# Low halves of w_down's split weights: a subtraction on VectorE, or a negated copy on ScalarE and an accumulating DMA

## The chip, the cores and the metric

One core of a Trainium2 chip runs one launch of the kernel. The metric is the device time of that launch in microseconds (us), median of three runs; the engines are TensorE (PE), VectorE (DVE), ScalarE (ACT), GpSimd (POOL) and SyncE (SP), and SP issues all DMAs of the kernel before.

## What is computed

One decoder layer for 512 prompt tokens and 64 sample tokens (576 columns in all, D_MODEL 1024, D_FF 4096). Only the last two lines matter here:

```python
h1 = x + jnp.concatenate([oa, ob], axis=-1) @ w_o
hid = jnp.square(jax.nn.relu(rmsnorm(h1, norm2_g) @ w_up))
y = h1 + hid @ w_down
```

All inputs and outputs are float32. The kernel multiplies in the type `fp32r`, which keeps fewer bits, and so splits each operand into a high part (the value rounded to `fp32r`) and a low part (the value minus its high part). A product is three matmuls: high by high, high by low, low by high.

## The kernel before

Matrices lie transposed: 128 features on the partitions, tokens along the free dimension, in two halves of 288 (`HALF`). One matmul is 128x128 weights by 288 tokens.

The whole kernel is written as generators (tasks) that a planner, `Flow`, interleaves at build time: `fl.op` books an instruction on an engine with a cost in ns, and the engine queues get their instructions in the order of the planned start times. The planner's costs set the order only; on the chip semaphores decide when each instruction starts.

The last stage is the MLP. `order` (L372 to L376) lists its weight groups: sixteen units `("u", u)` of w_up, and from u = 3 on, behind every odd u, the four chunks `("d", c, i)` of a block c of w_down (behind u = 15 the eight chunks of c = 6 and 7). A d chunk is 128 x 1024 floats (512 KB) and serves four k tiles by 256 output features. So there are seven places at which PE goes from a u unit to a run of d chunks, with 32 d chunks in all.

How a weight chunk reaches PE:

- `loader` (L393) issues its DMA from SP into a raw tile (`wr` in the profile, use `mr`, at most four at a time in this stage).
- `group_splitter` (L421) walks through `order` and takes tiles of the use `mw`, of which six may live at a time (L337). A product of a u unit takes one tile, which holds both parts of a 128 x 512 sum of blocks; a d chunk takes two, `h` and `l`, and only when it has both does it start `whole` (L485). `rel("mr")` and `rel("mw")` hand tiles back.
- `whole` writes the high part on ACT (`act(h, x)`), the low part on DVE (`tt(l, x, f(h), OP.subtract)`), marks the pair in `wready`, and frees the raw tile.
- `mlp_gemm` (L1888) is PE's program: for a u unit of u >= 2 the seven products of `up` (L1803) in the order `PO` = 1, 2, 6, 5, 7, 3, 4 of 12 matmuls each, for a d chunk two times `gemm` (L1006), 48 matmuls.

`gemm` uses the parts of a chunk in this order, so the low part is first read by the third matmul:

```python
mm(p, wh[:, s], x_h[:, j, c0:c1], j == 0, False, extra=extra)
mm(p, wh[:, s], x_l[:, j, c0:c1], False, False, extra=extra)
mm(p, wl[:, s], x_h[:, j, c0:c1], False, j == nk - 1, extra=extra)
```

In a u unit, ACT also copies the accumulators out after products 1, 6 and 5 (`up_out`, L1832, rows `uq<-pg`), and product 3 may start to accumulate onto product 5's accumulator only when that copy is done (`seen`, L1764, used at L1811). Products 3 and 4 end the unit.

With six `mw` tiles, the tiles of the first d chunk of a run are those of products 2 and 6 of the unit ahead; so its `h` can be written when product 6 is done, and products 5, 7, 3 and 4 (48 matmuls) stand between that and the chunk's own first matmul.

Of the kernel before, what the change touches and what calls it, by code (L numbers as in the profile page):

```python
# [13 lines left out]
OP = mybir.AluOpType  # L14
# [198 lines left out]
def hymba_step(ctx: ExitStack, tc: tile.TileContext, a):  # L213
    nc = tc.nc
    fl = Flow()
# [21 lines left out]
    def rel(*uses):  # L237
        def go():
            for u in uses:
                live[u] -= 1  # L240
                live[home[u]] -= 1
        fl.do(go)
# [5 lines left out]
    def size(x):  # L248
        n = 1
        for q in x.shape[1:]:  # L250
            n *= q
        return n
# [14 lines left out]
    def act(out, in_, func=AF.Copy, bias=0.0, scale=1.0, accum=None, mark=None, extra=0):  # L267
        cost = (51 if on_psum(in_) else 93) + size(in_) / 1.2 + extra
        cost += (93 if accum is not None else 0) + (93 if ap(bias) or ap(scale) else 0)
        fl.op("ACT", cost, lambda: nc.scalar.activation(out, in_, func, bias=bias, scale=scale,  # L270
                                                        accum_out=accum), mark)

    def dve(emit, out, in_, extra=0, fast=False, mark=None):
        fast = fast and not on_psum(out) and not on_psum(in_)
        fl.op("DVE", 68 + size(in_) / (1.92 if fast else 0.96) + extra, emit, mark)

    def tt(out, x, y, op, mark=None):
        dve(lambda: nc.vector.tensor_tensor(out, x, y, op=op), out, x, mark=mark)  # L278
# [41 lines left out]
    def dma(dst, src, mark=None, slow=1):  # L320
        fl.op("SP", 4 * slow * size(dst) * dst.shape[0] / 360.0, lambda: nc.sync.dma_start(dst, src), mark)  # L321

    go_on = lambda t: None

    f = lambda t: t.bitcast(F32)
# [32 lines left out]
    items, chunk, ready = [], {}, {}  # L358
# [43 lines left out]
    def mark(d, k, v):  # L402
        c = fl.cur
        fl.do(lambda: d.update({k: (v, c.t)}))
# [7 lines left out]
    wready = {}  # L412
# [8 lines left out]
    def group_splitter():  # L421
        yield lambda: "split_o" in done
        for g in order:
# [8 lines left out]
            if g[0] == "d":  # L432
                h = yield from get("mw", MID, "mw", F32R)
                l = yield from get("mw", MID, "mw", F32R)
                fl.spawn(whole(g, r[0], h, l))
                yield 0
                continue
# [46 lines left out]

    def whole(g, x, h, l):  # L485
        act(h, x)
        yield 0
        tt(l, x, f(h), OP.subtract)
        mark(wready, (g, 0), (h, l))
        rel("mr")  # L490
        yield 0

    def weights(g, k):
# [1547 lines left out]
```

## Time and profile before

| | us |
|---|---|
| median of 3 runs (816.64 to 821.53) | 818.16 |
| the profiled execution: its own time | 818.95 |
| its span, first to last instruction | 817.2 |
| PE busy | 792.2 (97%) |
| DVE busy | 568.7 (70%) |
| ACT busy | 348.3 (43%) |
| POOL busy | 109.4 (13%) |
| DMA queue of SP, share of 16 engines | 36.6% |

The profile page shows the span in 40 slices of 20.4 us, each digit the busy share of a slice in tenths; the rows of the groups below give a line of the kernel (L262 is the helper that issues every matmul, L270 every ScalarE instruction, L278 every two-operand VectorE instruction, L321 every DMA of SP), the operation, and the tile written and read. In the chain of waits each step is followed back to what released it. A row of the timeline merges equal instructions that follow each other; `[0.22 <-PE pg L262]` at its end says how long the engine was idle before it and what ended that. PE's clock was granted in full in the slices of the MLP.

### The profile page before, as it was taken

The page shows a single profiled execution, that of the slowest core. Times are in us where ns is not written, and L with a number is a line of the kernel's source. Part 1 is how long each engine was busy: PE and PEld are TensorE (multiplying, and loading weights), DVE is VectorE, ACT ScalarE, POOL GpSimd, SP SyncE. Part 2 cuts the span into 40 slices and gives each one's busy share as a digit, 9 for nine tenths or more (in the row PEclk, how much of TensorE's full clock was granted, in tenths as well). Part 3 has the DMA queues.
Part 4 walks back from the last instruction along what each step waited for, and adds up shares of the span by engine and source line. Part 5 has one row for each costly group of instructions (what it writes and reads, how often), then busy time and mean ns, then how long its engine had stood idle before and what let it go on. Part 6 is the DMA issues. An engine that isn't in the chain of part 4 may idle for free.

```text
span 817.2 us, 15699 instructions
## 1 busy us (share of the span) xinstructions
PE 792.2 (97%) x6323; PEld 728.1 (89%) x6323; DVE 568.7 (70%) x1250; ACT 348.3 (43%) x728; POOL 109.4 (13%) x128
## 2 busy tenths in 40 slices
PE   8989998999999999999997999999999999999998
PEld 8968877879778687778997999999999999999998
DVE  4366269888776785668798886768677676867642
ACT  5547453655242134443466543515343351534400
POOL 3443224134224000121000000000000000000000
PEclk9999999999999999999999999999999999999999
DMA  7732320106686799122221141404123130412302
GB/s 270 125 112 77 123 68 31 55 27 245 211 345 185 273 319 327 49 93 81 104 104 52 59 150 52 129 27 155 53 94 113 52 129 27 155 53 95 112 30 87
DMA packets 49864, 99.05 MB, mean 121 GB/s; under 512 B 12864, under 2 KB 26304, under 8 KB 49792
## 3 DMA queue, kind: packets, MB, share of 16 engines
q1 hardware_dynamic: 49792, 98.05, 36.6%
q8 instruction: 50, 0.82, 0.4%
q14 instruction: 22, 0.18, 0.1%
HBM read 88.15 MB, written 9.69 MB: 120 GB/s over the span
## 4 chain that ended last, share of the span: by engine, by line
PE 73%; issue 9%; DVE 7%; DMA 6%; ACT 2%; SPq 2%; POOL 1%; POOLq 0%; ACTq 0%; DVEq 0%
PE pg L262 53%; PE pa L262 7%; DVE y L285 2%; SPq L321 2%; PE cha L262 2%; DMA wr<-in_wk_dram 2%; DMA morekv<-in_cv_dram 1%; PE os L262 1%; PE ptp L265 1%; DMA morekv<-in_ck_dram 1%; PE cs L262 1%; DMA silvz<-dU 1%; PE sc L262 1%; PE s L262 1%; PE sn L262 1%
## 5 line engine op out<-in xcount | busy, mean ns | idle before, releaser
L262 PE MATMUL pg<-hid,mw 128*128 128x288 f32 x1536 | 204.7, 295 | 0.0
L262 PEld LDWEIGHTS pg<-hid,mw 128*128 128x128 f32 x1536 | 203.9, 188 | 0.0
L262 PE MATMUL pg<-xf,mw 128*128 128x288 f32 x1368 | 186.0, 297 | 4.6 <-ACT xf L270 3.8
L262 PEld LDWEIGHTS pg<-xf,mw 128*128 128x128 f32 x1368 | 183.7, 189 | 5.6 <-ACT xf L270 4.3
L278 DVE TENSOR_TENSOR h<-pg,h 128x288 f32<-128x288 f32 x160 | 72.5, 455 | 94.6 <-PE pg L262 93.8
L270 ACT ACTIVATE mw<-wr 128x512 fp32r<-128x512 f32 (+1 forms) x82 | 62.9, 791 | 70.8 <-PE pg L262 70.1
L262 PE MATMUL pg<-xh,wh 128*128 128x288 f32 x256 | 78.0, 305 | 0.0
L262 PE MATMUL pg<-xl,wh 128*128 128x288 f32 x256 | 78.0, 305 | 0.0
L262 PE MATMUL pg<-xh,wl 128*128 128x288 f32 x256 | 77.9, 304 | 0.0
L278 DVE TENSOR_TENSOR mw<-wr,mw 128x512 fp32r<-128x512 f32 (+1 forms) x82 | 72.4, 893 | 6.7 <-ACT mw L270 6.3
L270 ACT ACTIVATE mw<-ws 128x512 fp32r<-128x512 f32 x56 | 33.7, 627 | 45.3 <-PE pg L262 26.6
L262 PEld LDWEIGHTS pg<-xh,wh 128*128 128x128 f32 x256 | 48.4, 189 | 3.2 <-issue 3.0
L262 PEld LDWEIGHTS pg<-xh,wl 128*128 128x128 f32 x256 | 48.4, 189 | 2.8 <-issue 2.4
L262 PEld LDWEIGHTS pg<-xl,wh 128*128 128x128 f32 x256 | 48.5, 189 | 2.5 <-issue 1.9
L308 POOL TENSOR_TENSOR wl<-wr,wh 128x1024 fp32r<-128x1024 f32 x15 | 35.9, 2393 | 81.6 <-ACT wh L270 65.0
L262 PE MATMUL pa<-wh,xh 128*128 128x260 f32 (+1 forms) x128 | 43.1, 344 | 1.0 <-ACT wh L270 1.0
L262 PE MATMUL pa<-wh,xl 128*128 128x260 f32 (+1 forms) x128 | 43.6, 348 | 0.5 <-DVE xl L285 0.4
L262 PE MATMUL pa<-wl,xh 128*128 128x260 f32 (+1 forms) x128 | 42.7, 341 | 0.0
L270 ACT ACTIVATE wh<-wr 128x1024 fp32r<-128x1024 f32 (+1 forms) x40 | 38.6, 964 | 8.0 <-DMA wr<-in_wk_dram 5.1
L270 ACT ACTIVATE uq<-pg 128x288 f32<-128x288 f32 x42 | 17.1, 408 | 58.0 <-PE pg L262 58.0
L285 DVE SCALAR_TENSOR_TENSOR y<-u,cp,y 128x600 f32<-128x600 f32 x36 | 37.1, 1032 | 5.9 <-ACT u L270 3.3
L278 DVE TENSOR_TENSOR wl<-wr,wh 128x1024 fp32r<-128x1024 f32 (+1 forms) x25 | 28.4, 1134 | 16.0 <-ACT wh L270 15.9
(295 smaller groups left out, 1311.1 us busy)
## 6 DMA issues: line engine op xcount, KB each, us to landing
wr<-in_wu_dram SPq DMA_DIRECT2D x32, 512.0 KB, 3.3
wr<-in_wd_dram SPq DMA_DIRECT2D x32, 512.0 KB, 3.3
morekv<-in_ck_dram SPq DMA_DIRECT2D x20, 512.0 KB, 5.4
morekv<-in_cv_dram SPq DMA_DIRECT2D x20, 512.0 KB, 5.3
wr<-in_wb_dram SPq DMA_DIRECT2D x16, 512.0 KB, 4.0
wr<-in_wo_dram SPq DMA_DIRECT2D x8, 512.0 KB, 6.1
xr<-in_xT_dram SPq DMA_DIRECT2D x8, 288.0 KB, 5.6
h<-in_xT_dram SPq DMA_DIRECT2D x8, 288.0 KB, 7.2
```

The costliest lines, as they stand in the source:

```text
L262: lambda: nc.tensor.matmul(out, lhsT, rhs, start=start, stop=stop, skip_group_check=True))
L265: fl.op("PE", (97, 230), lambda: nc.tensor.transpose(out, in_, ident[:k, :k]))
L270: fl.op("ACT", cost, lambda: nc.scalar.activation(out, in_, func, bias=bias, scale=scale, accum_out=accum), mark)
L278: dve(lambda: nc.vector.tensor_tensor(out, x, y, op=op), out, x, mark=mark)
L285: dve(lambda: nc.vector.scalar_tensor_tensor(out, x, s, y, op0=op0, op1=op1), out, x, 61 if ap(s) else 0, mark=mark)
L308: fl.op("POOL", (135 + size(x) / 0.47) * slow, lambda: nc.gpsimd.tensor_tensor(out, x, y, op=op), mark)
L321: fl.op("SP", 4 * slow * size(dst) * dst.shape[0] / 360.0, lambda: nc.sync.dma_start(dst, src), mark)
```

## The change

```diff
+    def dma_add(dst, src, mark):
+        fl.op("POOL", 1100, lambda: nc.gpsimd.dma_start(dst, src, accum_op=OP.add), lambda t: mark(t + 3500))
...
     def whole(g, x, h, l):
         act(h, x)
-        yield 0
-        tt(l, x, f(h), OP.subtract)
-        mark(wready, (g, 0), (h, l))
         rel("mr")
+        act(l, f(h), scale=-1.0)
+        yield 0
+        dma_add(l, items[chunk[g + (0,)]][0], lambda t: wready.update({(g, 0): ((h, l), t)}))
         yield 0
```

For each of the 32 d chunks ScalarE writes the high part `h` as before, then writes its negative into `l`, and a DMA issued from GpSimd's queue reads the chunk a second time from HBM (`in_wd_dram`) and adds it to `l`, which then holds the weight minus its high part. The subtraction on VectorE is gone, and the raw tile is free after the first ScalarE instruction. The planner books the DMA as 1100 ns on POOL and 3500 ns more until `l` can be used. Lines below the new helper move down by three.

How the instructions move, at the second of the seven places where a run of d chunks follows a u unit. On **ScalarE**, around the end of the unit (`uq<-pg` copies product 6 and then 5 out; `mw<-wr 128x1024` is a chunk's high part), before:

```order
L270 ACTIVATE uq<-pg 128x288 [waits PE_49]
L270 ACTIVATE mw<-wr 128x1024 [waits DMAHW4_49]
L270 ACTIVATE uq<-pg 128x288 [waits PE_49]
L270 ACTIVATE mw<-wr 128x1024 [waits DMAHW5_49]
L270 ACTIVATE mw<-wr 128x1024 [waits DMAHW6_49,PE_49]
L270 ACTIVATE uq<-uq 128x576 [waits DVE_49]
L270 ACTIVATE uq<-uq 128x576
L270 ACTIVATE hid<-uq 128x2x288 [waits Activation_49] x2
L270 ACTIVATE mw<-wr 128x1024 [waits DMAHW7_49,PE_49]
```

and now, where `mw<-mw 128x1024` is the negated copy:

```order
L270 ACTIVATE uq<-pg 128x288 [waits PE_49]
L270 ACTIVATE mw<-wr 128x1024 [waits DMAHW4_49]
L270 ACTIVATE mw<-mw 128x1024 [waits DVE_49,Activation_49]
L270 ACTIVATE uq<-pg 128x288 [waits PE_49]
L270 ACTIVATE mw<-wr 128x1024 [waits DMAHW5_49]
L270 ACTIVATE mw<-mw 128x1024 [waits Activation_49]
L270 ACTIVATE mw<-wr 128x1024 [waits DMAHW6_49,PE_49]
L270 ACTIVATE uq<-uq 128x576 [waits DVE_49]
L270 ACTIVATE uq<-uq 128x576
L270 ACTIVATE hid<-uq 128x2x288 [waits Activation_49]
L270 ACTIVATE mw<-mw 128x1024 [waits PE_49]
L270 ACTIVATE hid<-uq 128x2x288 [waits Activation_49]
```

The first chunk's negated copy now stands ahead of the copy of product 5; the second chunk's follows its high part at once, and the third chunk's is put between the two `hid` rows. On POOL the 32 new DMAs stand behind everything that queue had. On **PE**, at the start of the first run, before:

```order
L262 MATMUL pg<-xf_4542,mw 128x288 x3
L262 MATMUL pg<-hid,mw 128x288 x48
L262 MATMUL pg<-hid,mw 128x288 [waits Activation_49]
L262 MATMUL pg<-hid,mw 128x288
L262 MATMUL pg<-hid,mw 128x288 [waits DVE_49]
```

and now:

```order
L262 MATMUL pg<-xf_4542,mw 128x288 x3
L262 MATMUL pg<-hid,mw 128x288 x2
L262 MATMUL pg<-hid,mw 128x288 [waits DMASW0_49]
L262 MATMUL pg<-hid,mw 128x288 x45
L262 MATMUL pg<-hid,mw 128x288 [waits Activation_49]
L262 MATMUL pg<-hid,mw 128x288
L262 MATMUL pg<-hid,mw 128x288 [waits DMASW1_49]
```

The order of the matmuls is the same; the third matmul of each chunk now waits for the landing of the chunk's DMA (`DMASW`). On **SP**, the loads around the same place as in the rows of ScalarE (the raw chunks of the next two u units), before:

```order
L321 DMA wr<-in_wu_dram 128x1024 [waits DMAHW3_49,DMAHW0_49,DVE_49]
L321 DMA wr<-in_wu_dram 128x1024 [waits DMAHW4_49,DVE_49]
L321 DMA wr<-in_wu_dram 128x1024 [waits DMAHW5_49,DMAHW2_49,DVE_49]
L321 DMA wr<-in_wu_dram 128x1024 [waits PE_49]
L321 DMA wr<-in_wd_dram 128x1024 [waits DVE_49,PE_49] x2
```

and now:

```order
L321 DMA wr<-in_wu_dram 128x1024 [waits DMAHW0_49,PE_49]
L321 DMA wr<-in_wu_dram 128x1024 [waits DMAHW4_49,Activation_49]
L321 DMA wr<-in_wu_dram 128x1024 [waits DMAHW5_49,DMAHW2_49,Activation_49]
L321 DMA wr<-in_wu_dram 128x1024 [waits DMAHW7_49,DMAHW3_49,Activation_49]
L321 DMA wr<-in_wd_dram 128x1024 [waits DVE_49,PE_49]
```

The second and third of these loads waited for VectorE's subtractions and now wait for ScalarE's high parts, which are earlier.

## Rows read from the trace of the kernel before

**Rows 1.** The page: busy time by engine, and PE and its clock in 40 slices
```profile
span 817.2 us, 15699 instructions
PE 792.2 (97%) x6323; PEld 728.1 (89%) x6323; DVE 568.7 (70%) x1250; ACT 348.3 (43%) x728; POOL 109.4 (13%) x128
...
PE   8989998999999999999997999999999999999998
...
PEclk9999999999999999999999999999999999999999
```

**Rows 2.** The chain of waits from 430 us on: start, length, what
```profile
443.15 370.65 PE pg L262 x2794
813.80 0.02 issue
813.83 0.46 DVE h L278
```

**Rows 3.** Timeline of PE in the MLP: start, us, engine line op xcount
```profile
443.08 33.51 PE L262 MATMUL pg<-xf,mw 128*128 128x288 f32 x250
476.43 25.60 PE L262 MATMUL pg<-hid,mw 128*128 128x288 f32 x192
501.87 22.44 PE L262 MATMUL pg<-xf,mw 128*128 128x288 f32 x168
524.15 25.60 PE L262 MATMUL pg<-hid,mw 128*128 128x288 f32 x192
549.59 22.44 PE L262 MATMUL pg<-xf,mw 128*128 128x288 f32 x168
571.87 25.60 PE L262 MATMUL pg<-hid,mw 128*128 128x288 f32 x192
...
762.75 51.04 PE L262 MATMUL pg<-hid,mw 128*128 128x288 f32 x384
```

**Rows 4.** Groups by line and shape, 400 to 820 us: busy, mean ns, idle before
```profile
L278 DVE TENSOR_TENSOR mw<-wr,mw 128x1024 fp32r<-128x1024 f32 x32 | 39.0, 1218 | 4.5 <-ACT mw L270 4.5
L270 ACT ACTIVATE mw<-wr 128x1024 fp32r<-128x1024 f32 x32 | 33.7, 1054 | 13.5 <-PE pg L262 12.8 <-DVE mw L278 0.7
```

**Rows 5.** Busy time by engine, one d run and the next u units
```profile
524.15:549.59 25.44, 25.44 (x195) 25.44 (x193) 15.56 (x29) 6.92 (x11) 0.00 (x0) 1.00 0.13 42
549.59:571.87 22.28, 22.28 (x171) 22.28 (x169) 18.29 (x32) 12.10 (x21) 0.00 (x0) 1.00 0.44 142
```

**Rows 6.** Timeline of ACT: high parts of the first chunk, first and last run
```profile
470.57 1.05 ACT L270 ACTIVATE mw<-wr 128x1024 fp32r<-128x1024 f32 x1
...
756.89 1.05 ACT L270 ACTIVATE mw<-wr 128x1024 fp32r<-128x1024 f32 x1
```

**Rows 7.** Timeline of ACT around the start of a run at 571.87
```profile
565.71 0.41 ACT L270 ACTIVATE uq<-pg 128x288 f32<-128x288 f32 x1 [1.06 <-PE pg L262]
566.01 1.05 ACT L270 ACTIVATE mw<-wr 128x1024 fp32r<-128x1024 f32 x1
567.29 0.41 ACT L270 ACTIVATE uq<-pg 128x288 f32<-128x288 f32 x1 [0.22 <-PE pg L262]
567.59 1.05 ACT L270 ACTIVATE mw<-wr 128x1024 fp32r<-128x1024 f32 x1
568.87 1.06 ACT L270 ACTIVATE mw<-wr 128x1024 fp32r<-128x1024 f32 x1 [0.22 <-PE pg L262]
572.56 1.26 ACT L270 ACTIVATE uq<-uq 128x576 f32<-128x576 f32 x2 [2.63 <-DVE uq L285]
```

**Rows 8.** Timeline of DVE there: the first chunk's subtraction
```profile
567.10 1.23 DVE L278 TENSOR_TENSOR mw<-wr,mw 128x1024 fp32r<-128x1024 f32 x1 [0.76 <-ACT mw L270]
```

**Rows 9.** DMA issues of the whole kernel: KB each, median us to landing
```profile
wr<-in_wd_dram SPq DMA_DIRECT2D x32, 512.0 KB, 3.3
...
h<-in_xT_dram SPq DMA_DIRECT2D x8, 288.0 KB, 7.2
out_yT_dram<-h SPq DMA_DIRECT2D x16, 144.0 KB, 1.8
...
wr<-in_wk_dram SPq DMA_DIRECT2D x4, 512.0 KB, 12.3
```

**Rows 10.** Timeline of SP's queue, 566.5 to 569 us
```profile
568.35 0.33 SPq L321 DMA_DIRECT2D wr<-in_wu_dram  x1
```

More of the change, by code (lines that the diff above doesn't have):

```diff
@@ L486, in whole @@
         act(h, x)
+        rel("mr")
+        act(l, f(h), scale=-1.0)
         yield 0
-        tt(l, x, f(h), OP.subtract)
-        mark(wready, (g, 0), (h, l))
-        rel("mr")
+        dma_add(l, items[chunk[g + (0,)]][0], lambda t: wready.update({(g, 0): ((h, l), t)}))
         yield 0
```

## The prediction

> **What bounds the kernel now.** I read the page first: PE is busy for 792.2 of 817.2 us at its full clock [rows 1], so other engines matter only where PE waits for them. The chain of waits then shows the part that the change touches: from 443.15 us to the end it is one unbroken piece, PE's matmuls for 370.65 us, and only the last addition on VectorE behind it [rows 2]. The timeline of PE says how tight that is. A run of 192 matmuls on d chunks starts at 524.15 and the next u unit at 549.59, which is 132.5 ns a matmul; the 168 matmuls of the next two units take 22.28 us, 132.6 ns each [rows 3]. The pace does not change where one kind of work follows the other, so PE waits for no weight in this stage: every split is early enough. The reader should see two things: VectorE's subtractions are nowhere on the path, and any new wait of PE adds to the time one for one, because nothing behind it can make it up.
>
> **What is removed.** 32 subtractions of 1218 ns, 39.0 us of VectorE's time [rows 4]. I cost this at nothing: PE's own work hides it. VectorE is busy 18.29 of 22.28 us beside the u units and 15.56 of 25.44 beside the d run [rows 5], and PE waits for it in neither.
>
> **What ScalarE gets.** 32 copies of 1024 columns from SBUF to SBUF. The nearest row is its copy of the same shape, 1054 ns [rows 4]; a factor of -1 changes nothing that I can see there. That is 33.7 us more. In a period of a d run and two units ScalarE works 6.92 + 12.10 us [rows 5]; four copies make it 23.2 of 47.7 us, so it has room. One place is tight. The first chunk's negated copy now stands ahead of the copy of product 5, which ran at 567.29 for 0.41 us, released by PE 0.22 us before [rows 7], so product 5 ended near 567.07. The negated copy can start at about 567.1 and ends at 568.15, so that copy ends at about 568.6 instead of 567.7. Product 3, which needs it, starts after the 12 matmuls of product 7: 567.07 + 1.59 = 568.66. It just fits. If it missed by 0.1 us, PE would lose that ahead of the chunk instead of inside it, and the wait priced next would be shorter by as much, so I add nothing for it.
>
> **What PE now waits for.** This is the term that counts. At 571.87 PE starts a run [rows 3]. The first chunk's high part is written from 566.01 to 567.06 [rows 7]; it cannot be earlier, since its tiles come free with product 6. VectorE's subtraction started 0.04 us behind it and was done at 568.33 [rows 8], 3.8 us before the low part was read. In the new order the negated copy takes that place: 567.10 + 1.05 = 568.15, and GpSimd can issue the DMA from 568.19 on (the same 0.04 us). PE reads the low part with its third matmul, at 571.87 + 2 x 0.1325 = 572.14. **The DMA has 3.95 us from the earliest issue to its landing.** The lead of 5.86 us from high part to run is the same at the first run (470.57 to 476.43) and the last (756.89 to 762.75) [rows 3, 6], and at those between: seven times in all.
>
> How long does this DMA take? No row shows one from GpSimd's queue, nor one that adds. Bounds from the rows: a plain load of the same 512 KB from the same tensor, issued by SP, lands 3.3 us after its issue, and nothing speaks for an accumulating one being quicker [rows 9]. From above I take 7.2 us, the slowest loads into this second half of the kernel, which stood in a crowded queue [rows 9]. Between them: 512 KB need 3.3 us and 144 KB 1.8 us [rows 9], so 1.5 us for 368 KB, which makes about 2.1 us of data and 1.2 us of fixed time. An accumulating DMA must also bring the old contents of `l` to the adder. If that is a second pass of the same length, it takes 1.2 + 2 x 2.1 = 5.4 us. That is the value I take, because it rests on the row of the same bytes and on what the operation must do. The Trainium skill says of such transfers (DMA: Bandwidth & Descriptors, Rules for kernel authors) that the accumulate reads its destination and writes it later; no run here shows it yet, and it speaks for the second pass.
>
> PE then waits 5.4 - 3.95 = 1.45 us at each of seven starts: **10.2 us**. At the lower bound the wait is zero, at the upper 7 x 3.25 = 22.8 us.
>
> The other 25 chunks I cost at nothing. The second chunk's negated copy follows at about 568.6 + 2 x 1.05 = 570.7, and its low part is read at 572.14 + 48 x 0.1325 = 578.5: 7.8 us, more than the upper bound. The third chunk's copy stands between the `hid` rows, behind the squares at 572.56 [rows 7], at about 575.5 at the latest, against 584.9. The fourth and the run of eight at the end have two whole chunks (12.7 us) or nearly that.
>
> **What moves on the queues.** The second u load, which waited for the subtraction and left at 568.35 [rows 10], now waits only for the high part and can leave at about 567.1, so it moves its last bytes while the new DMA starts. At 3.3 us from issue [rows 9] it is over by 570.4; some tenths of a microsecond are in this, inside my bounds. The DMA engines have room: their share is 0.44 beside the units and 0.13 in the run [rows 5], and four more transfers per period beside eight do not fill it. GpSimd has nothing else to do in this stage (0.00 busy [rows 5]).
>
> **The sum.** The profiled execution took 818.95 us with a span of 817.2; that is 0.8 above the median of 818.16. 818.95 + 10.2 = 829.1, or 828.4 against the median. That is 1.2% more; a measurement of this kernel can tell about 0.5% (4.1 us) from no change, which is 0.58 us per start, a DMA of 4.5 us.
>
> **Rivals.**
>
> *The DMA fits into its 3.95 us (up to 4.5 us counts as no change).* For it: the plain load at 3.3 us [rows 9] leaves 0.65 us, and an adder that reads both sides at once would need no second pass. Against it: the issue itself by GpSimd, the second operand, and the load beside it. The time would be 818.2, at most 822. The Trainium skill has a fit for plain copies from GpSimd's queue (DMA: Bandwidth & Descriptors, Anatomy of one DMA), 2.0 us plus the bytes over 436 GB/s; as an estimate that gives 3.2 us here, no wait, and this rival's time. The 3.3 us of SP's loads agree with it, but neither number is of a DMA that adds.
>
> *The accumulate is slow.* If the adder takes the data at a fraction of the rate, a DMA lasts over 7.2 us. The first chunk's wait then carries the later chunks along, since they have 4 us more. With the slowest row of this kernel, 12.3 us [rows 9], it is 7 x 8.35 = 58 us, 876 us. Nothing in the trace excludes it; the rows that are so slow come from a full queue, and this one is not full.
>
> *VectorE's relief speeds PE up.* This is the case on the other side. It would need PE's matmuls to be slowed by VectorE's traffic in SBUF. The place to see it is the pace: with VectorE busy 82% of the time (units) a matmul takes 132.6 ns, with 61% (d run) 132.5 [rows 3, 5]. The relief is 39.0 of 370.65 us, 10.5 points, so 0.05 ns on some 2800 matmuls, 0.1 us. It would decide only if the DMA also landed within 3.95 us, and then reach 0.5% only at a pace lower by 1.5 ns. The time would be 814 or less.
>
> That the change doesn't take place can be left out: the order shows the 32 DMAs and PE's waits for them.
>
> **How the numbers follow.** A wait of 0.58 to 3.25 us per start, around 1.45: 0.62. The DMA fits: 0.22. Slow accumulate, over 841: 0.11. Faster: 0.05. Slower is thus 0.73. The range goes from the lowest run of before, 816.6, which takes in the case of no change, to 818.16 + 22.8 = 841; it leaves out the slow accumulate and the faster case.
>
> **What would show it.** Right: in the timeline of PE the runs of d chunks start with two matmuls and then a gap of 0.6 to 3.3 us, released by a DMA, at seven places and no others; the u stretches keep 22.28 us; the DMA issues list `mw<-in_wd_dram` x32 with 4.5 to 7.2 us to landing. Wrong: no gap with a landing under 4 us (the first rival); gaps at second or third chunks too, or a gap over 3.3 us (the second); gaps ahead of product 3, which would say that ScalarE is the tight place; or a matmul pace other than 132.5 ns.

## The result and the profile after

The changed kernel takes 855.68 us in the median of its runs (849.72 to 862.90), the kernel before 817.40 beside it. The ratio is 1.0434, with a 95% interval of 1.0348 to 1.0521; it leaves out the run of 862.90 us, which the comparison sets aside as disturbed, while the median does not. The forecast was 828.4 us, and its range ended at 841.0: the sign and the place were right, the size was not.

The profiled execution took 859.07 us with a span of 857.3, 40.1 us more than the 817.2 of [rows 1]. The page of the changed kernel answers to [rows 1, 4 and 9]:

```profile
span 857.3 us, 15828 instructions
...
PE 805.0 (94%) x6323; PEld 740.1 (86%) x6323; DVE 532.9 (62%) x1218; ACT 379.3 (44%) x760; POOL 137.5 (16%) x160
...
q0 software_dynamic: 4608, 16.78, 10.8%
...
L262 PE MATMUL pg<-hid,mw 128*128 128x288 f32 x1536 | 215.9, 303 | 29.8 <-DMA mw<-in_wd_dram 29.8
...
wr<-in_wu_dram SPq DMA_DIRECT2D x32, 512.0 KB, 5.3
wr<-in_wd_dram SPq DMA_DIRECT2D x32, 512.0 KB, 3.6
mw<-in_wd_dram POOLq DMA_DIRECT2D x32, 512.0 KB, 7.5
```

VectorE lost its 32 instructions and gave nothing back, as [rows 2] had said it would. The line to read is that of the d matmuls: 29.8 us of idle time in front of them, all ended by the new DMA. The same line shows a second thing that is easily passed over: the mean matmul lasts 303 ns, though the matmuls are the same. In the kernel before the line was:

```profile
L262 PE MATMUL pg<-hid,mw 128*128 128x288 f32 x1536 | 204.7, 295 | 0.0
```

The last line of the changed kernel gives the landing of the new DMAs, 7.5 us in the median, beyond the 7.2 us that the prediction had as its upper bound.

The timeline of PE in the MLP, with the columns of [rows 3] (the rows left out repeat the pattern):

```profile
442.06 33.51 PE L262 MATMUL pg<-xf,mw 128*128 128x288 f32 x250
475.41 0.43 PE L262 MATMUL pg<-hid,mw 128*128 128x288 f32 x2
482.02 26.77 PE L262 MATMUL pg<-hid,mw 128*128 128x288 f32 x190 [6.19 <-DMA mw<-in_wd_dram]
508.64 22.44 PE L262 MATMUL pg<-xf,mw 128*128 128x288 f32 x168
530.92 0.42 PE L262 MATMUL pg<-hid,mw 128*128 128x288 f32 x2
534.97 26.97 PE L262 MATMUL pg<-hid,mw 128*128 128x288 f32 x190 [3.63 <-DMA mw<-in_wd_dram]
...
694.88 25.44 PE L262 MATMUL pg<-hid,mw 128*128 128x288 f32 x190 [3.11 <-DMA mw<-in_wd_dram]
...
800.68 53.19 PE L262 MATMUL pg<-hid,mw 128*128 128x288 f32 x382 [4.72 <-DMA mw<-in_wd_dram]
```

Each of the seven runs of d chunks now begins with two matmuls and a gap; the gaps are 6.19, 3.63, 3.16, 5.43, 3.11, 3.59 and 4.72 us. There is no other gap, and the u stretches keep their 22.44 us. But behind six of the seven gaps the run itself is longer: 190 matmuls take 26.76 to 26.97 us in five of these, the 382 of the last run 2.31 us more than at the old pace, and behind the fifth gap 190 take 25.44.

The 40.1 us then add up as follows.

| part | us | from |
|---|---|---|
| seven gaps | 29.8 | the sum above |
| matmuls that run slower behind a gap | 9.4 | 1.33 + 1.53 + 1.42 + 1.32 + 0 + 1.52 over 25.44, and 53.19 - 50.88 in the last run (50.88 is 25.44 and 192 x 0.1325) |
| matmuls that no longer overlap across a gap (one lasts 0.295 us, one starts every 0.1325) | 1.9 | 7 x 0.27: two pieces of 0.43 + 25.44 us where one of 25.60 stood [rows 3] |
| the stage starts earlier | -1.0 | 442.06 against 443.08 [rows 3] |

**Why the DMA is late.** POOL's timeline ahead of the second of these starts, at 530.92:

```profile
527.50 0.87 POOL L324 DMA_DIRECT2D mw<-in_wd_dram  x1 [35.60 <-ACT uq L270]
529.84 0.86 POOL L324 DMA_DIRECT2D mw<-in_wd_dram  x1 [1.47 <-ACT mw L270]
```

and the timeline of SP's queue in the same stretch:

```profile
526.14 0.33 SPq L321 DMA_DIRECT2D wr<-in_wu_dram  x1
528.47 0.33 SPq L321 DMA_DIRECT2D wr<-in_wu_dram  x1
```

The first chunk's DMA is issued at 527.50 and must have landed at 531.19 (530.92 and two matmuls); it landed 7.4 us after its issue. Two loads of SP stand around it. Counted from the start of the run they leave 4.78 and 2.45 us ahead of it. Before the change the same two loads left 3.52 us (568.35, [rows 10], against 571.87) and 0.82 us ahead. Both waited for VectorE's subtractions; now they wait for ScalarE's high parts only. The second chunk's own DMA joins them 1.08 us ahead of the run. So four transfers of 512 KB overlap: the loads land after 4.1 and 6.6 us, the two accumulating DMAs after 7.4 and 7.6. The two loads don't weigh alike. At its old time, 3.52 us ahead of the run, the first would leave just ahead of the DMA (issued 3.42 us ahead), so by this arithmetic leaving earlier takes it out of the DMA's way rather than into it; the second moves from 0.82 to 2.45 us ahead, into the DMA's time. No run here moved one of the two alone against this kernel.

What the 16 DMA engines do meanwhile stands in the busy time by stretch (columns: the stretch, its length, busy time of PE, PEld, DVE, ACT and POOL, the granted clock of PE, the DMA share, GB/s). The first row runs from the DMA's issue to the moment at which it was due:

```profile
527.50:531.19 3.69, 3.69 (x29) 3.61 (x28) 1.91 (x5) 2.96 (x3) 1.73 (x2) 1.00 0.89 215
530.92:534.97 4.05, 0.42 (x5) 0.19 (x3) 0.46 (x1) 3.36 (x6) 0.29 (x1) 1.00 0.96 222
534.97:536.00 1.03, 1.03 (x8) 1.03 (x9) 0.00 (x0) 0.93 (x1) 0.57 (x1) 1.00 1.05 211
536.00:537.00 1.00, 1.00 (x7) 1.00 (x6) 0.23 (x1) 0.00 (x0) 0.00 (x0) 0.59 0.96 180
537.00:538.00 1.00, 1.00 (x6) 1.00 (x6) 0.90 (x2) 0.00 (x0) 0.00 (x0) 0.50 0.88 135
538.00:539.00 1.00, 1.00 (x6) 1.00 (x6) 0.00 (x0) 0.00 (x0) 0.00 (x0) 0.50 0.99 188
539.00:540.00 1.00, 1.00 (x7) 1.00 (x7) 0.35 (x1) 0.00 (x0) 0.00 (x0) 0.70 0.99 274
540.00:541.00 1.00, 1.00 (x10) 1.00 (x9) 0.78 (x2) 0.00 (x0) 0.00 (x0) 1.00 0.84 287
```

The DMA engines are full here, where the means of [rows 5] had said 0.44 and 0.13 (the view counts a packet in the stretch in which it starts, so a share can pass 1). Two rows say how that comes about. The first is the corresponding stretch of the kernel before, up to the third matmul of the run at 571.87; the second is an accumulating DMA with no other transfer beside it, from the kernel under "The DMA entirely by itself" below:

```profile
568.45:572.14 3.69, 3.69 (x30) 3.69 (x30) 2.95 (x6) 1.26 (x2) 0.00 (x0) 1.00 0.51 152
...
527.08:532.39 5.31, 3.84 (x29) 3.60 (x28) 2.29 (x5) 4.17 (x7) 0.86 (x1) 1.00 0.61 99
```

0.51 was in use in this place already, and the DMA wants 0.61 for itself: 1.12, as an estimate, even before any load moves.

**Why the matmuls are slower** is in the rows above: PE stood still until 534.97, and from about 536 on its granted clock is 0.50 (1.2 GHz) for some three microseconds. PE is busy all the time, but the run takes 1.53 us longer than 25.44. (The counts, 6 matmuls in a microsecond against 10 at 1.00, which is 2.4 GHz, take in those that lie in the stretch only in part; they are no rates.) The clock doesn't always fall so late. In the first gap, from 475.84 to 482.02, it falls while PE stands still:

```profile
478.00:479.00 1.00, 0.00 (x0) 0.00 (x0) 0.00 (x0) 1.00 (x2) 0.00 (x0) 0.58 1.13 238
```

### The profile page after: what moved, and what is told of

Read it like the earlier page. It is cut to its first block, busy times and chain, and to the rows that moved or that the text cites. A ratio compares the mean times of both kernels' runs of the same rounds, so it can differ in the third digit from the quotient of the medians.

```text
span 857.3 us, 15828 instructions
## 1 busy us (share of the span) xinstructions
PE 805.0 (94%) x6323; PEld 740.1 (86%) x6323; DVE 532.9 (62%) x1218; ACT 379.3 (44%) x760; POOL 137.5 (16%) x160
## 3 DMA queue, kind: packets, MB, share of 16 engines
q0 software_dynamic: 4608, 16.78, 10.8%
## 4 chain that ended last, share of the span: by engine, by line
PE 53%; issue 25%; DVE 9%; DMA 6%; ACT 4%; POOL 1%; SPq 1%; POOLq 0%; ACTq 0%
PE pg L262 32%; PE pa L262 8%; DMA mw<-in_wd_dram 3%; DVE y L285 2%; PE cha L262 1%; DMA wr<-in_wk_dram 1%; PE ptp L265 1%; SPq L321 1%; PE sn L262 1%; PE cs L262 1%; PE sc L262 1%; PE os L262 1%; ACT mw L270 1%; DMA wr<-in_wu_dram 1%; ACT wh L270 1%
## 5 line engine op out<-in xcount | busy, mean ns | idle before, releaser
L262 PE MATMUL pg<-hid,mw 128*128 128x288 f32 x1536 | 215.9, 303 | 29.8 <-DMA mw<-in_wd_dram 29.8
L262 PEld LDWEIGHTS pg<-hid,mw 128*128 128x128 f32 x1536 | 213.6, 196 | 31.4 <-DMA mw<-in_wd_dram 31.4
L324 POOL DMA_DIRECT2D mw<-in_wd_dram x32 | 28.1, 877 | 350.7 <-ACT uq L270 210.1
L270 ACT ACTIVATE mw<-mw 128x1024 fp32r<-128x1024 f32 x32 | 33.8, 1056 | 50.1 <-PE pg L262 49.6
```

The lines of the kernel that those rows point to most:

```text
L262: lambda: nc.tensor.matmul(out, lhsT, rhs, start=start, stop=stop, skip_group_check=True))
L324: fl.op("POOL", 1100, lambda: nc.gpsimd.dma_start(dst, src, accum_op=OP.add), lambda t: mark(t + 3500))
```

## The experiments

The theory after this reading had three parts: the DMA is late because SP's loads, released early, and the second accumulating DMA share the DMA engines with it; its own length is as forecast; and the idle PE loses its clock. The rivals were that an accumulating DMA is slow by itself, that ScalarE's part costs something, and that the matmuls run slower because of the DMA traffic instead of PE's idleness. Every kernel was timed beside the kernel before on the same chip; that one's medians were 819.65 us (the first four kernels below), 818.0 (the kernel with a gap but no DMA, and the last one) and 818.2 (the other four).

### SP's loads held back until the DMA has landed

A copy of eight columns of the landed `l`, issued by SP, stands ahead of the release of the first chunk's raw tile.

```diff
         act(h, x)
-        rel("mr")
+        if g[2]:
+            rel("mr")
...
+        if not g[2]:
+            yield lambda: (g, 0) in wready
+            dma(held, f(l[:, :8]), go_on)
+            rel("mr")
```

> SP holds the u loads back until the first accumulating DMA of a run has landed; the second accumulating DMA still moves beside it. If the u load is the main neighbour, the first DMA lands after 5.1 to 5.8 us and the time is 827 to 835. If the second accumulating DMA is, it lands after 6.5 to 7.5 us and the time is 840 to 850.

Measured: 832.11 us, ratio 1.0137 (1.0100 to 1.0174). The first DMA of each run lands after 5.3 to 5.6 us, though the second DMA still follows it 2.3 us later. From PE's timeline, two of its seven gaps:

```profile
529.79 25.44 PE L262 MATMUL pg<-hid,mw 128*128 128x288 f32 x190 [1.51 <-DMA mw<-in_wd_dram]
...
778.05 52.40 PE L262 MATMUL pg<-hid,mw 128*128 128x288 f32 x382 [1.80 <-DMA mw<-in_wd_dram]
```

The gaps are 1.50 to 1.80 us, 11.6 in all, and only the last run is slow (52.40 against 50.88). This is the kernel that the prediction described: a DMA of 5.4 us, a wait of 1.45 us, 10.2 us in all. SP's loads beside it are what makes the DMA late. The kernel holds them back until behind the landing, later than they left before the change (530.37 and 531.03 at the second start, where the run begins at 527.86), so it does not show what their leaving early adds.

### The DMA entirely by itself

As above, and GpSimd also waits for each DMA to land before it issues the next.

```diff
         dma_add(l, items[chunk[g + (0,)]][0], lambda t: wready.update({(g, 0): ((h, l), t)}))
+        yield lambda: (g, 0) in wready
+        pool_cp(seen1, f(l[:, :8]), go_on)
```

> Each accumulating DMA moves alone: GpSimd waits for its landing before it issues the next, and SP holds the u loads back until the first one of a run has landed. Theory (the wait is long because the first DMA of a run shares the 16 DMA engines with the second one and with a u load): the first DMA of a run lands after 5.1 to 5.4 us, like the undisturbed ones of the changed kernel, PE waits 1.4 to 1.8 us at each of seven starts, 10 to 12 us in all, and the time is 827 to 830, or up to 840 if the clock still falls after each gap. Rival (the first DMA of a run is slow by itself, whatever moves beside it): it lands after 7 to 9.7 us as in the changed kernel, and the time stays near 850.

Measured: 856.2 us, ratio 1.0453 (1.0399 to 1.0506). The landing was as expected, 5.3 to 5.5 us at all seven starts, and the time was not: the second chunk's DMA now leaves late, runs into the loads that SP lets go at that moment, and lands after 7.1 to 9.3 us. The third run, from PE's timeline:

```profile
583.47 6.62 PE L262 MATMUL pg<-hid,mw 128*128 128x288 f32 x48 [1.58 <-DMA mw<-in_wd_dram]
592.88 20.62 PE L262 MATMUL pg<-hid,mw 128*128 128x288 f32 x142 [2.78 <-DMA mw<-in_wd_dram]
```

Each start has two gaps, 26.0 us in all. The isolation moved the collision from the first chunk to the second. What the run does settle is the first row: with no other transfer beside it the wait is 1.50 to 1.72 us, so the second DMA alone adds next to nothing to it.

### Accumulating DMAs for the first chunks only

The other three chunks of each block go back to VectorE's subtraction, by which SP's second early load also goes back to its old time (0.82 us ahead of the run).

```diff
     def whole(g, x, h, l):
+        if g[2]:
+            act(h, x)
+            yield 0
+            tt(l, x, f(h), OP.subtract)
+            mark(wready, (g, 0), (h, l))
+            rel("mr")
+            yield 0
+            return
```

> Only the first chunk of each run is split with the accumulating DMA, the other 25 by VectorE. So the first DMA moves beside a u load alone. If the u load is the main neighbour, the DMA lands after 6.5 us or more and the time stays at 840 to 850. If the second accumulating DMA is, it lands after 5.1 to 6 us, PE waits 1.5 to 2.3 us at seven starts, and the time is 827 to 835.

Measured: 848.57 us, ratio 1.0348 (1.0301 to 1.0394). The first DMA lands after 5.6 to 7.4 us, the gaps are 3.92, 1.82, 1.76, 2.52, 3.26, 2.02 and 2.12, 17.4 us in all. The time is what was expected if the load is the main neighbour, but only two of the landings (7.4 and 7.1 us) are over the 6.5 us that went with it. Two of the gaps, from PE's timeline:

```profile
530.85 26.98 PE L262 MATMUL pg<-hid,mw 128*128 128x288 f32 x190 [1.82 <-DMA mw<-in_wd_dram]
...
686.75 25.45 PE L262 MATMUL pg<-hid,mw 128*128 128x288 f32 x190 [3.26 <-DMA mw<-in_wd_dram]
```

So of the 29.8 us some 11 to 12 are the DMA's own length, 5.8 more (17.4 - 11.6) come with the one load that still leaves early and the other at its old time, and the remaining 12.4 (29.8 - 17.4) need that other load's early start and the second DMA as well. This split is rough, since each sum is of one execution: the profiled one took 836.07 us against a median of 832.11 with SP's loads held back, 844.89 against 848.57 here, and 859.07 against 855.68 in the changed kernel. By the ratios to the kernel before, 1.0137, 1.0348 and 1.0434, the first of the two steps is the larger one. What holds either way is that the second DMA without the loads costs next to nothing and the loads without it do cost. The two rows show something that the theory had not: behind 1.82 us of idleness the run lost 1.5 us to the clock, behind 3.26 us nothing. The length of a gap alone doesn't say whether the clock falls.

### A plain copy in place of the accumulation

The DMA overwrites `l` instead of adding to it, which leaves the subtraction out.

```diff
-        fl.op("POOL", 1100, lambda: nc.gpsimd.dma_start(dst, src, accum_op=OP.add), lambda t: mark(t + 3500))
+        fl.op("POOL", 1100, lambda: nc.gpsimd.dma_start(dst, src), lambda t: mark(t + 3500))
```

> The same DMA from GpSimd's queue without the addition: the low part becomes the weight itself instead of the weight minus its high part, so this kernel leaves the subtraction out. If the addition is what makes the DMA long, it lands after 3.5 to 4.5 us, PE waits under 1 us per start, and the time is 815 to 823. If it is GpSimd's queue, it lands after 6 us or more, as the accumulating one does, and the time is 840 to 855.

Measured: 845.31 us, ratio 1.0313 (1.0270 to 1.0356). Undisturbed copies land after 3.5 to 3.6 us, the first of a run after 4.4 to 7.5, and the gaps come to 17.0 us. I had expected hardly any wait; even a plain copy is late behind the early loads. Two rows of its page:

```profile
q0 software_dynamic: 4608, 16.78, 6.4%
...
mw<-in_wd_dram POOLq DMA_DIRECT2D x32, 512.0 KB, 4.4
```

Adding costs time of its own, and the two pages price it. The queue of the 32 transfers takes 10.8% of 857.3 us in the changed kernel, 92.6 us of 16 engines, and 6.4% of 847.8 us as plain copies, 54.3: 1.7 times as much for the same bytes. Undisturbed, the accumulating DMA lands after 5.1 to 5.3 us (the fourth chunks of the changed kernel) against 3.5 to 3.6, so adding takes some 1.6 us. A plain copy of 3.6 us by itself would fit into the time that is there (3.69 us at the second start), so the 17.0 us of gaps are the price of its company alone. With the addition the company costs about as much: 29.8 - 11.6 = 18.2 us.

### VectorE's subtraction for the first chunks

The opposite of accumulating for the first chunks only: the first chunk of each block keeps the old subtraction, the others go by DMA.

```diff
     def whole(g, x, h, l):
+        if not g[2]:
+            act(h, x)
+            yield 0
+            tt(l, x, f(h), OP.subtract)
+            mark(wready, (g, 0), (h, l))
+            rel("mr")
+            yield 0
+            return
```

> The first chunk of each run is split by VectorE as before, the other 25 by the accumulating DMA. Theory (only the first chunk of a run has too short a lead): PE has no gap at the start of a run, the second chunk has about 8.6 us for its DMA and waits at most 1.5 us where it shares the engines, the clock stays up, and the time is 815 to 822. Rival (DMAs that add cost PE time all through the stage, by traffic or by the order of the queues): 830 or more.

Measured: 817.96 us, ratio 0.9979 (0.9954 to 1.0004). PE's timeline has no gap, and its runs are those of [rows 3]:

```profile
521.09 25.60 PE L262 MATMUL pg<-hid,mw 128*128 128x288 f32 x192
```

24 of the 32 DMAs cost nothing (24 and not the 25 of the expectation, since the eighth block's first chunk, inside the last run, keeps VectorE too), and they land after 5.0 to 7.8 us. The whole loss belongs to the first chunks.

### ScalarE's part alone

ScalarE writes the negated copy, and VectorE adds the weight where the DMA did.

```diff
         act(h, x)
-        rel("mr")
         act(l, f(h), scale=-1.0)
         yield 0
-        dma_add(l, items[chunk[g + (0,)]][0], lambda t: wready.update({(g, 0): ((h, l), t)}))
+        tt(l, f(l), x, OP.add)
+        mark(wready, (g, 0), (h, l))
+        rel("mr")
```

> ScalarE writes the negative high part as in the changed kernel, but VectorE adds the weight, and no DMA does. If the 32 more ScalarE copies cost nothing, as forecast, the time is 815 to 820. If the copy that now stands ahead of the copy of product 5 holds PE up, there is a gap ahead of product 3 at seven places and the time is 821 or more.

Measured: 818.11 us, ratio 0.9992 (0.9966 to 1.0017), with no gap in PE's timeline. The 32 copies on ScalarE are free, the one that stands ahead of product 5's copy among them.

### A gap without a DMA

The kernel before, in which the subtraction of each run's first chunk is repeated until the low part is late. Nothing is added to the DMA queues.

```diff
         yield 0
-        tt(l, x, f(h), OP.subtract)
+        for n in range(1 if g[2] or g[1] == 7 else 6):
+            tt(l, x, f(h), OP.subtract)
```

> The kernel before, with VectorE's subtraction for the first chunk of each run done six times over instead of once (the last result is the same), so that PE waits 2.5 to 5 us at the same place, with no DMA and no ScalarE instruction changed. Theory (PE's idleness alone brings the clock down): at some of the seven starts the granted clock falls to its lower level behind the gap, those runs take 1.3 to 1.7 us longer than 25.4 us, and the time is 817 plus the gaps plus 3 to 11 us: 837 to 862. Rival (the DMA traffic brings it down): gaps, but every run at full clock and 25.4 us.

Measured: 864.52 us, ratio 1.0564 (1.0522 to 1.0607), 2.5 us above what I had expected at most. The first start, from PE's timeline:

```profile
482.37 27.69 PE L262 MATMUL pg<-hid,mw 128*128 128x288 f32 x190 [4.00 <-DVE mw L278]
```

and four stretches, the first inside the gap and the others behind it, with the columns of the stretches above:

```profile
480.50:481.50 1.00, 0.00 (x0) 0.00 (x0) 0.96 (x2) 1.00 (x3) 0.00 (x0) 0.53 0.00 0
482.37:484.00 1.63, 1.63 (x7) 1.63 (x8) 1.63 (x2) 0.00 (x0) 0.00 (x0) 0.50 0.41 98
...
486.00:487.00 1.00, 1.00 (x6) 1.00 (x5) 0.28 (x1) 0.00 (x0) 0.00 (x0) 0.50 0.00 0
...
488.00:489.00 1.00, 1.00 (x10) 1.00 (x9) 0.28 (x1) 0.00 (x0) 0.00 (x0) 1.00 0.00 0
```

The clock falls inside the gap while the DMA engines move nothing, is at 0.50 in the third row with no traffic either, and is back at 1.00 at 488. VectorE is busy for 0.28 us in both of the last two rows, so it makes no difference there. All seven gaps (3.84 to 4.00 us) are followed by slow runs; the first six take 27.69 to 28.20 us, 2.3 to 2.8 more than 25.44, where 1.3 to 1.7 had been expected at some of them. So the slower matmuls come from PE's standing still, not from the traffic.

### The gaps filled with other matmuls

24 matmuls on the high part, into an accumulator that nothing reads, stand ahead of each run's first chunk, at all seven starts (the expectation says six).

```diff
+                if not i and c < 7:
+                    pd = yield from get("g", [128, 288], "pd")
+                    for n in range(24):
+                        mm(pd, wh[:, :128], hid[c][:, 0, 0, :288], n == 0, n == 23, extra=8)
+                    rel("g")
+                    yield 0
```

> The changed kernel with 24 more matmuls (3.2 us) on the high part ahead of six of the seven runs, into an accumulator that nobody reads, so that PE works through the first part of each wait. Theory (the half clock behind a gap follows from PE's idleness, and the DMA sets when PE can go on): the gaps shrink by 3.2 us each, the 192 matmuls of a run take 25.3 to 25.5 us again, and the time falls by 6 to 11 us against the changed kernel in spite of the added work, to 844 to 850. Rival (the clock falls for another reason, the DMA traffic for one): runs still take 26.6 to 27 us and the time is 855 to 862.

Measured: 851.42 us, ratio 1.0381 (1.0323 to 1.0438), 1.4 us above the upper end of what was expected; two starts kept a gap of over 2 us. The gaps are 2.72, 0.33, 0.55, 0, 0, 2.19 and 0 us. From PE's timeline, one start of each kind:

```profile
484.31 26.97 PE L262 MATMUL pg<-hid,mw 128*128 128x288 f32 x190 [2.72 <-DMA mw<-in_wd_dram]
...
537.32 25.44 PE L262 MATMUL pg<-hid,mw 128*128 128x288 f32 x190 [0.33 <-DMA mw<-in_wd_dram]
```

Behind 2.72 and 2.19 us the run is slow, behind the others it has its full clock, with the same DMAs beside it. The filling itself keeps PE busy for 23.3 us, so nothing clear is won; but it confirms from the other side that PE's idleness brings the clock down.

### The low part read later

In each d chunk the 32 matmuls on the high part come first, for four accumulators, and the 16 on the low part after them; the planner's due time for a d chunk is put forward by 4200 ns. That gives the DMA 30 x 0.1325 = 4.0 us more.

```diff
-                for j in range(2):
-                    after = lambda hf, p, m=2 * i + j: add_down(m, hf, p, c == 7)
-                    yield from gemm(wh, wl, hid[c][:, 0], hid[c][:, 1], 4, 256, j * 128, after, extra=8)
+                for part in range(2):
+                    for j in range(2):
+                        for hf, (c0, c1) in enumerate(HALF):
...
+                                if not part:
+                                    mm(p, wh[:, s], hid[c][:, 0, k, c0:c1], k == 0, False, extra=8)
+                                    mm(p, wh[:, s], hid[c][:, 1, k, c0:c1], False, False, extra=8)
+                                else:
+                                    mm(p, wl[:, s], hid[c][:, 0, k, c0:c1], False, k == 3, extra=8)
```

> The changed kernel, with the matmuls of each w_down chunk in another order: the 32 that read the high part first, for all four accumulators, then the 16 that read the low part. So the DMA of a run's first chunk has 30 x 0.1325 = 4.0 us more, 7.7 us from its issue. With landings of 6.9 to 9.7 us, PE waits 0 to 2 us per start, 4 us in all, the clock stays up at most starts, and the time is 817 to 826. If the DMA then still decides, for instance since its landing moves back with it, the time stays over 835.

Measured: 823.37 us, ratio 1.0076 (1.0035 to 1.0116). The first DMA of the seven runs lands after 9.5, 6.5, 6.8, 6.4, 9.1, 6.0 and 9.0 us. With 3.7 + 4.0 = 7.7 us to spare, three of these are late, and PE's timeline has three gaps, of 2.07, 1.33 and 1.23 us, the first of them:

```profile
481.08 21.48 PE L262 MATMUL pg<-hid,mw 128*128 128x288 f32 x160 [2.07 <-DMA mw<-in_wd_dram]
```

Here 2.07 us of idleness cost no clock (160 x 0.1325 = 21.2).

### Both cures

SP's hold and the later reading together: the edits of the first and the ninth kernel above, the beginnings of which stand here.

```diff
-        rel("mr")
+        if g[2]:
+            rel("mr")
...
+                for part in range(2):
...
```

> The changed kernel with SP's hold on the u loads and the low products last. Theory (the whole loss is the first DMA's landing against PE's third matmul, and what hangs on it): the DMA lands after 5.3 to 5.6 us, 7.7 us are there, PE waits nowhere, and the time is 816 to 821, the same as before. Rival (something else in the change costs time, such as traffic all through the stage): 823 or more.

Measured: 819.13 us, ratio 1.0021 (0.9998 to 1.0044). The first DMAs land after 5.1 to 5.3 us, later ones after up to 11.9, and PE's timeline has no gap:

```profile
524.98 25.61 PE L262 MATMUL pg<-hid,mw 128*128 128x288 f32 x192
```

With the loads out of the DMA's way and its due time put back, the change costs nothing that can be measured. It gains nothing either: PE's runs are as long as in [rows 3], and no version of the ten beat the kernel before.

## Why the prediction was wrong

**What bounds the kernel, and what is removed**: right. PE's work is unbroken in this stage, so VectorE's relief was worth nothing; the matmul pace of the u stretches did not change, and where only the first chunks kept VectorE the time was 817.96 us.

**What ScalarE gets**: right. The copy that "just fits" ahead of product 5's does fit; 818.11 us with ScalarE's part alone.

**What PE now waits for**: the place was right, the third matmul of a run at seven starts and nowhere else, and so was the length of an undisturbed DMA, 5.4 us forecast and 5.1 to 5.6 measured. The second pass over the old contents, of which the estimate was made, would take the data twice; measured are 1.7 times the engine time. That the value fits so well is in part luck, since its two parts were off in opposite directions: the plain copy from GpSimd's queue takes 3.5 to 3.6 us where 3.3 was taken, and the addition some 1.6 where 2.1 was added. The Trainium skill's rule (DMA: Bandwidth & Descriptors, Rules for kernel authors) that the accumulate reads its destination before it writes it is in accord with these 1.7 times. The budget was 3.69 us instead of 3.95, since GpSimd began its issue 0.30 us behind the negated copy (527.20 to 527.50) instead of 0.04. The price of this step, 10.2 us, is near what the kernel with SP's loads held back shows: 11.6.

**What moves on the queues**: this is the step that failed. It said that one load would leave earlier, that "some tenths of a microsecond are in this, inside my bounds", and that "the DMA engines have room". There were three errors in it. The order on SP showed two loads whose waits changed from VectorE to ScalarE, and I priced one. I read the DMA engines' load as a mean over 22 us (0.44). In the 3.69 us in which the DMA has to land it was 0.51 before, the DMA by itself takes 0.61, and in the changed kernel it was 0.89 in that stretch and 0.96 in the wait behind it. And I left out that the second chunk's own DMA starts 2.3 us behind the first. The first DMA then landed after 6.9 to 9.7 us, and the gaps were 29.8 us instead of 10.2. The Trainium skill states (DMA: Bandwidth & Descriptors, Issuing engines are not separate DMA queues) that DMAs of all issuing engines run on the same 16 DMA engines and interleave. The trace agrees: load and accumulating DMA take 6.6 and 7.4 us beside each other, where 3.3 [rows 9] and 5.1 are their times alone.

**The upper bound** of 7.2 us came from the loads of a crowded queue, which move 288 KB without adding (and were issued at 311 to 323 us, not in the second half of the kernel). It was no bound for 512 KB that are added.

**The sum** lacked a term: 9.4 us of matmuls at half clock behind the gaps. I counted a wait of PE one for one, and here 29.8 us of gaps cost 41.1 us, with 9.4 for the clock and 1.9 for the lost overlap, 1.4 times their length.

**The rivals.** "The accumulate is slow" had landings over 7.2 us, which five of the seven are, but not for its reason: the adder costs some 1.6 us, the company the rest. Its further sign, that the first chunk's wait carries later chunks along, did not appear. That the DMA fits is excluded by the 5.1 us it takes alone; that VectorE's relief speeds PE up, by the pace.

**Open**: what decides whether the clock falls behind a given gap. It fell behind 1.76 us and not behind 3.26 in the same execution. And how the loss that the company makes divides between the two loads' early starts and the second DMA, which were not tried one by one.

## What to carry to other kernels

Price a transfer in the few microseconds in which it has to land, with everything else that the same edit releases there; a mean DMA share over a stage does not show it (0.44 in the mean, 0.51 in that place before the change, and 0.61 more for the new transfer), and freeing a buffer earlier can move its next load into that place. A wait of a saturated PE can cost more than its length (here 1.4 times), because the clock may fall with it. And in a run of similar items look at the first: PE waited for seven of the 32 DMAs, those at the starts of its runs, and for no other.

## What the runs showed of the hardware

- An accumulating DMA of 512 KB from HBM, issued by GpSimd, lands 5.1 to 5.6 us after its issue when nothing competes, a plain copy from the same queue 3.5 to 3.6, SP's load 3.3 [rows 9]; the issue takes GpSimd 0.87 us with the addition (877 ns in the mean of 32) and 0.54 without. Among other transfers the accumulating one took up to 11.9 us.
- Behind gaps of PE of 1.76 to 6.19 us matmuls ran at half clock for some three to six microseconds, at a price of 1.3 to 2.8 us; but not behind each of them (not behind 2.02, 2.07, 3.11 and 3.26 us, for instance). In some gaps the clock fell while PE still stood (at about 478.2, ahead of 482.02, in the changed kernel), at other starts up to 1.4 us after PE had begun again (at about 747.8 against 746.46).
- A lone accumulating DMA of 512 KB kept the 16 DMA engines 0.61 busy from its issue to its landing.
